# Later column products for two modulation groups, and two slices of the first modulation summed on VectorE

## The chip, the cores and the metric

The kernel runs on one core of a Trainium2 chip. The core has five engines with queues of their own: TensorE (PE, matrix products into PSUM), VectorE (DVE) and ScalarE (ACT) for elementwise work, GpSimd (POOL), and SyncE (SP), whose queue issues the loads and stores here. PE's weight loads are listed apart, as PEld. An engine takes its instructions in the order of its queue, and an instruction that waits holds up all behind it. The metric is the device time of one execution in microseconds (us); smaller is better.

## The reference

One layer of a streaming encoder: a feed-forward block, a token mixer, a second feed-forward block. Each is fed a modulated input, and its result comes back through a gate. All nine modulation vectors are one product of SiLU(c) with `w_ada` (1024 x 9216). x is 512 x 1024, the inner width of a feed-forward is 2816, everything is float32.

```python
sc = jax.nn.silu(c)
mod = sc @ w_ada[l] + b_ada[l]
sh1, s1, g1, sh2, s2, g2, sh3, s3, g3 = jnp.split(mod, N_MOD, axis=-1)
h = _modulate(x, sh1, s1)                       # _rms(x) * (1 + s1) + sh1
x = x + 0.5 * g1[:, None, :] * _swiglu(h, ffn1_w_in[l], ffn1_w_out[l])
h = _modulate(x, sh2, s2)
y = _hybrid_mixer(h, ...)
x = x + g2[:, None, :] * y
h = _modulate(x, sh3, s3)
x = x + 0.5 * g3[:, None, :] * _swiglu(h, ffn2_w_in[l], ffn2_w_out[l])
```

`_swiglu(h, w_in, w_out)` is `(silu(gate) * up) @ w_out` with gate and up the two halves of `h @ w_in`.

## The kernel before, in words

The activations lie transposed in the 128 partitions: eight tiles of 128 channels x 512 tokens. A full-precision product is made of three matmuls on split operands: high x high (L448), low x high (L449) and high x low (L450), 128 x 512 each. Weights come as raw tiles `wr`; ACT casts them to the high part `wh` (L217), DVE subtracts for the low part `wl` (L218). The same split of the modulated input gives `hh` (ACT, L649) and `hl` (DVE, L636), from `hm` (DVE, L647). A unit is one 128-column tile of weights against all eight input tiles: 24 matmuls. A pair of units (gate and up) makes one of 22 tiles f of the inner width.

The first feed-forward begins with phase 0. There the modulation that it needs itself (sh1, s1) is not known yet, and PE makes it as it goes. For each of the eight channel tiles kt there is a slice of `w_ada` of 1 MB (`ar`, 128 x 8 x 2 x 128, two loads) and a weight tile of 384 KB. In group kt, PE first makes the raw columns of kt + 1: small matmuls of 32 columns, packed side by side in the array (`phase0_cols`, L598), which leave partial sums in four partition bands. ACT copies them to `sg` (L601), and two matmuls against a selector, `sel4`, add the bands up into a column each for shift and scale (`columns`, L516). DVE adds the bias (L517, L518) and makes `hm` and `hl` of tile kt + 1, ACT makes `hh`. Between these stand the products of group kt into six accumulators (three tiles f, gate and up). All engines' instructions in phase 0 are tied to the order of the code (`in_order`); elsewhere a scheduler orders them, and the order below is what it gave.

The other modulation groups are summed by DVE beside the products: `ada_rest` loads rows of `w_ada`, scales them by SiLU(c) and adds them up into accumulators `aa` of 128 x 512 (L770 for the first, L772 for each further row tile). What then remains is a sum over partitions. `ada_columns` does it on PE with matmuls against ones, up to four side by side in the array (L791), has ACT copy the result, and transposes it (L798) so that DVE can add the bias (L802) and shift gates (L809). `ada_rest` is a generator, stepped by its caller, `side.step`, after each piece of a product.

- In the first feed-forward, group 0 (g1 and sh2) is stepped through tiles f = 3 to 6, and flushed at the end of f = 6, so its L791 stand there. f = 7 follows, a plain tile with another side job, and then come the products by sevens (L336), which take fewer but combined operands (`tl`, `th`, `sf`, made by DVE and ACT beforehand).
- In the last down projection, group 3 (the last gate; two accumulators) is stepped three times for each part of an output tile. Each of the eight tiles t has three parts (K of 8, 8 and 6 tiles). Tiles 0 and 1 are held in PSUM until the gate is there, then finished (L932), and tile 0 is stored (L1013).

SP issues the loads in order, with at most eight under way; a load also waits until its buffer is free.

Of the kernel before, what the change touches and what calls it, by code (L numbers as in the profile page):

```python
# [11 lines left out]
F32 = mybir.dt.float32  # L12
# [7 lines left out]
P = 128  # L20
# [8 lines left out]
KPARTS = ((0, 8), (8, 8), (16, 6))  # L29
SEVEN = range(8, 19), range(4, 19)  # L30


# [35 lines left out]
class Rates:  # L68


    def __init__(self, sides, rates):
        self.sides, self.rates, self.at = sides, rates, 0

    def step(self, n=1):
# [15 lines left out]
class Block:  # L90
# [51 lines left out]
    @contextmanager  # L142
    def in_order(self, ends=None):

        with self.traced() as block:
            yield
        self.ends = dict(ends or {})
        for i in block:
            if i.engine in self.ends:
                self.follow(i, self.ends[i.engine])  # L150
            self.ends[i.engine] = i.name
# [326 lines left out]
    def phase0(self):  # L478
# [4 lines left out]
        ss = self.const([P, 2 * NB], s="ss")  # L483
        loads = [self.phase0_load(0), self.phase0_load(1)]
        pv = self.aux()
# [26 lines left out]

        def columns(kt, sg, pg):
            k = slice(kt, kt + 1)
            for m in range(2):
                nc.tensor.matmul(pg[:, 256 + m:257 + m], sg[:, m * P:m * P + P], self.sel4, start=True, stop=True)  # L516
            nc.vector.tensor_tensor(out=self.c1[:, k], in0=pg[:, 256:257], in1=self.vT[:, k], op=ALU.add)  # L517
            nc.vector.scalar_tensor_tensor(out=self.c2[:, k], in0=pg[:, 257:258], scalar=1.0, in1=self.vT[:, 8 + kt:9 + kt],  # L518
                                           op0=ALU.add, op1=ALU.add)

        def weights(kt):
            raw, hi, lo = loads[kt][1]
            self.split_w(raw[:, :6, :], hi[:, :6, :], lo[:, :6, :])
            return hi, lo
# [6 lines left out]
        dg = self.diag(r)  # L531
        cols = self.phase0_cols(0, loads[0][0])
        raw0, wh, wl = (x[:, :6, :] for x in loads[0][1])
        w = wh, wl
# [13 lines left out]
        raw(*tiles[7])  # L548
        pu = [self.acc() for _ in range(3)] + [self.aux() for _ in range(3)]
        for kt in range(KT):  # L550
            (hi, lo), (xh, xl) = w, self.h[kt]
            more = kt + 1 < KT
            if kt + 2 < KT:
                loads.append(self.phase0_load(kt + 2))
            if kt == 0:
# [20 lines left out]

    def phase0_load(self, kt):
        a1, win = self.ins["w_ada"][0], self.ins["ffn1_w_in"][0]
        a = self.p0.tile([P, KT, 2, P], F32, tag="ar", name=self.name("ar"))
        w = self.w_tiles()  # L580

        def ada():
            for m in range(2):
                self.load(a[:, :, m, :], a1[:, m * D + kt * P:m * D + (kt + 1) * P].rearrange("(k p) n -> p k n", p=P))

        ada()
        self.loaded = self.load(w[0][:, :6, :].rearrange("p (m j) f -> p m (j f)", m=2),
                  win[kt * P:(kt + 1) * P, :].rearrange("p (m f) -> p m f", m=2)[:, :, :384])
        return a, w

    def phase0_cols(self, kt, a):
# [9 lines left out]
        nc.scalar.copy(sg, pg[:, :256])  # L601
        return sg, pg

# [140 lines left out]
    def ada_rest(self, groups, late=False):  # L744
# [98 lines left out]
    def ffn1(self):  # L843
# [81 lines left out]
    def down(self, act, gate, norm=None):  # L925
# [34 lines left out]
        for t in range(last):  # L960
            if norm and t == 1:
                self.masks()
            for i, _ in enumerate(parts(t, full, late=not norm and t < 2)):
                side.step(2 if norm else 3)
                if t > 2:
                    consts.step()
                if not norm and i == 1 and t > 2:
                    self.store(t - 2, range(NB))
            if not norm and t == 1:
                side.flush()  # L970
                for h in held:
                    finish(*h)
                self.store(0, range(NB))
        side.flush()
# [1158 lines left out]
```

## Time and profile before

| | |
|---|---|
| device time, median of 3 | 1056.32 us (1053.74 to 1056.46) |
| profiled execution | 1056.87 us, span 1055.2 us |
| mean granted TensorE clock | 0.997 |
| PE busy | 1034.8 us, 98% |
| DVE busy | 719.2 us, 68% |
| ACT busy | 487.1 us, 46% |
| PE busy from 60 to 90 us / 90 to 130 / 930 to 955 | 30.00 of 30 / 39.07 of 40 / 23.37 of 25 |
| DVE busy in the same stretches | 25.16 / 34.64 / 14.83 |

Phase 0 lies in the first 60 us, the ones-products of group 0 at 110 to 113 us, those of group 3 at 942 to 946 us. A row of a timeline reads: start in us, duration in us, engine, line, operation, output and inputs, shape and count; in brackets the idle time ahead of it and what ended it. Matmuls overlap in the trace, so the distance between two starts is what one of them costs PE, not its duration. A row of the waits reads: engine and line that waited, what it waited for, us in total, number of waits, longest.

### The profile page before, as it was taken

How to read it: one execution, taken by the hardware profiler on the slowest of the kernel's cores; microseconds unless marked ns; L12 is line 12 of the kernel's file. 1: busy time of each engine (PE TensorE's matmuls, PEld its weight loads, DVE VectorE, ACT ScalarE, POOL GpSimd, SP SyncE). 2: the span in 40 equal slices, each digit the busy share in tenths (PEclk: the TensorE clock that was granted, in tenths of full speed). 3: DMA queues.
4: the chain of work that ended last, by engine and by line, in shares of the span. 5: the costliest groups of instructions: out<-in, count | busy, mean ns of one | idle time of the engine just before them, and what ended most of it. 6: DMA issues, size and time to landing. Idle time of an engine off the chain costs nothing.

```text
span 1055.2 us, 16491 instructions
## 1 busy us (share of the span) xinstructions
PE 1034.8 (98%) x6489; PEld 906.8 (86%) x6489; DVE 719.2 (68%) x1278; ACT 487.1 (46%) x890; POOL 24.9 (2%) x74
## 2 busy tenths in 40 slices
PE   6999999999999999999999989999999999999998
PEld 5788799998887798888788769998999999878888
DVE  4479888767687937558788477788788886663221
ACT  3453455556222225568865554364555556512221
POOL 0000000000000000100000001100000000000000
PEclk8999999999999999999999999999999999999999
DMA  9988333334888635311232021104333344373311
GB/s 275 286 259 274 87 101 104 104 97 127 265 277 276 191 90 161 86 41 41 61 75 71 21 80 41 40 23 119 96 105 101 101 120 118 114 229 92 112 57 40
DMA packets 208028, 130.75 MB, mean 124 GB/s; under 512 B 13889, under 2 KB 192078, under 8 KB 207950
## 3 DMA queue, kind: packets, MB, share of 16 engines
q1 hardware_dynamic: 207950, 129.69, 41.5%
q8 instruction: 51, 0.84, 0.3%
q14 instruction: 27, 0.22, 0.1%
HBM read 127.18 MB, written 2.49 MB: 123 GB/s over the span
## 4 chain that ended last, share of the span: by engine, by line
PE 88%; DVE 6%; issue 2%; DMA 2%; ACT 1%; POOL 0%; SPq 0%; POOLq 0%; ACTq 0%; DVEq 0%
PE pa L448 17%; PE pa L449 16%; PE pa L450 16%; PE pa L336 14%; PE pb L336 11%; DVE aa L772 1%; DMA ar<-in_w_ada 1%; PE pb L1866 1%; PE pb L1846 1%; PE pb L598 1%; PE pb L448 1%; PE pb L449 1%; PE pb L450 1%; PE pb L1466 1%; DVE wl L218 1%
## 5 line engine op out<-in xcount | busy, mean ns | idle before, releaser
L217 ACT CAST wh<-wr 128x1024 fp32r<-128x1024 f32 (+1 forms) x112 | 112.1, 1006 | 221.2 <-PE pa L449 192.9
L218 DVE TENSOR_TENSOR wl<-wr,wh 128x1024 fp32r<-128x1024 f32 (+1 forms) x112 | 130.4, 1168 | 110.8 <-ACT wh L217 106.2
L448 PE MATMUL pa<-hh,wh 128*128 128x512 f32 (+1 forms) x421 | 162.3, 385 | 0.0
L450 PE MATMUL pa<-hh,wl 128*128 128x512 f32 (+1 forms) x421 | 160.4, 381 | 0.0
L449 PE MATMUL pa<-hl,wh 128*128 128x512 f32 (+1 forms) x421 | 160.4, 381 | 0.0
L448 PE MATMUL pa<-ah,wh 128*128 128x512 f32 (+1 forms) x396 | 146.6, 370 | 0.0
L450 PE MATMUL pa<-ah,wl 128*128 128x512 f32 (+1 forms) x396 | 145.4, 367 | 0.0
L449 PE MATMUL pa<-al,wh 128*128 128x512 f32 (+1 forms) x396 | 145.1, 366 | 0.0
L448 PEld LDWEIGHTS pa<-hh,wh 128*128 128x128 f32 x421 | 79.4, 189 | 16.5 <-issue 1.7
L450 PEld LDWEIGHTS pa<-hh,wl 128*128 128x128 f32 x421 | 79.3, 188 | 14.5 <-DVE wl L218 0.4
L449 PEld LDWEIGHTS pa<-hl,wh 128*128 128x128 f32 x421 | 79.4, 189 | 13.1 <-DVE hl L636 0.2
L448 PEld LDWEIGHTS pa<-ah,wh 128*128 128x128 f32 x396 | 74.7, 189 | 14.2 <-ACT wh L217 2.5
L450 PEld LDWEIGHTS pa<-ah,wl 128*128 128x128 f32 x396 | 74.7, 189 | 13.0 <-issue 0.8
L252 DVE TENSOR_TENSOR wl<-sf,wh 128x1024 fp32r<-128x1024 f32 x52 | 63.5, 1221 | 31.7 <-ACT wh L256 31.6
L449 PEld LDWEIGHTS pa<-al,wh 128*128 128x128 f32 x396 | 74.8, 189 | 11.8
L772 DVE SCALAR_TENSOR_TENSOR aa<-ar,sc,aa 128x512 f32<-128x512 f32 x98 | 73.0, 749 | 10.1 <-DMA ar<-in_w_ada 8.6
L336 PE MATMUL pa<-hh,wl 128*128 128x256 f32 x208 | 59.0, 284 | 0.0
L336 PE MATMUL pa<-tl,wh 128*128 128x256 f32 x208 | 59.0, 284 | 0.0
L336 PE MATMUL pa<-th,wl 128*128 128x256 f32 x208 | 59.0, 284 | 0.0
L336 PE MATMUL pa<-th,wh 128*128 128x256 f32 x208 | 59.0, 283 | 0.0
L336 PE MATMUL pa<-hh,wh 128*128 128x256 f32 x208 | 59.0, 283 | 0.0
L336 PE MATMUL pa<-hl,wh 128*128 128x256 f32 x208 | 59.0, 283 | 0.0
(435 smaller groups left out, 2290.3 us busy)
## 6 DMA issues: line engine op xcount, KB each, us to landing
wr<-in_ffn_w_in SPq DMA_DIRECT2D x79, 512.0 KB, 3.9
ar<-in_w_ada SPq DMA_DIRECT2D x80, 256.0 KB, 5.5
ar<-in_w_ada SPq DMA_DIRECT2D x32, 512.0 KB, 6.4
wr<-in_ffn_w_out SPq DMA_DIRECT2D x32, 512.0 KB, 4.1
wr<-in_w_in SPq DMA_DIRECT2D x21, 512.0 KB, 3.7
wr<-in_ffn_w_out SPq DMA_DIRECT2D x16, 384.0 KB, 3.6
wr<-in_w_out SPq DMA_DIRECT2D x8, 512.0 KB, 4.0
wr<-in_ffn_w_in SPq DMA_DIRECT2D x8, 384.0 KB, 8.3
```

What stands on the lines that cost most here:

```text
L217: self.nc.scalar.copy(hi, raw)
L218: self.nc.vector.tensor_tensor(out=lo, in0=raw, in1=hi.bitcast(F32), op=ALU.subtract)
L252: sub = lambda out, x, y: nc.vector.tensor_tensor(out=out, in0=x, in1=y, op=ALU.subtract)
L336: nc.tensor.matmul(z, a[:, j, :], b, start=start and j == 0 and i == 0, stop=j == 3 and i == 2, skip_group_check=not start)
L448: mm(out, wh, xh, start=start, stop=False)
L449: mm(out, wh, xl, start=False, stop=False)
L450: mm(out, wl, xh, start=False, stop=stop)
L598: nc.tensor.matmul(pg[32 * q:32 * q + 32, :256], self.sc[:, kc:kc + 1].to_broadcast([P, 32]), a[:, kc], start=(e == 0), stop=(e == 1), til ...
L772: nc.vector.scalar_tensor_tensor(out=acc, in0=a, scalar=sc, in1=acc, op0=ALU.mult, op1=ALU.add)
L1466: nc.tensor.matmul(pa[:, ps], kh[:, ps], x[:, ps], start=True, stop=True)
L1846: nc.tensor.matmul(ps[:, :n], self.qnT[h][:, ts], self.knT[h][:, :n], start=True, stop=False)
L1866: nc.tensor.matmul(po[:, :P], pT[:, b * P:(b + 1) * P], v[b][:, h * P:(h + 1) * P], start=(b == 0), stop=(b == i))
```

## The change

It has three parts. Line numbers of the changed kernel are higher than those before: L448, L449, L450 become L453, L454, L455; L798 becomes L830, L791 becomes L823; L636 and L647 become L665 and L676; L217 and L218 become L222 and L223.

Part A, phase 0. The slice of a group is loaded one step ahead of its weights. For slices 5 and 7 the matmuls of `phase0_cols` and the copy after them are left out; instead ACT scales the first row tile of the slice (L626) and DVE adds the other seven (L628), 128 x 256 each, and `columns` uses ones for the selector. These are not tied to the order of the code. `columns` of the other slices comes one product earlier in its group, that of the summed ones ahead of the group's first product.

SP's queue from slice 2 on, before (`ar` are slices, `wr` weights):

```order
L128 DMA ar78_262<-in_w_ada 128x8x128 x2
L128 DMA wr79_263<-in_ffn1_w_in 128x2x384
L128 DMA ar87_312<-in_w_ada 128x8x128 x2
L128 DMA wr88_313<-in_ffn1_w_in 128x2x384
L128 DMA ar94_358<-in_w_ada 128x8x128 x2
L128 DMA wr95_359<-in_ffn1_w_in 128x2x384
```

The same queue after, from slice 2 on:

```order
L130 DMA ar24_122<-in_w_ada 128x8x128 x2
L130 DMA ar79_265<-in_w_ada 128x8x128 x2
L130 DMA wr80_268<-in_ffn1_w_in 128x2x384
L130 DMA ar88_315<-in_w_ada 128x8x128 x2
L130 DMA wr89_318<-in_ffn1_w_in 128x2x384
L130 DMA ar95_361<-in_w_ada 128x8x128 x2
```

Slice 3 has moved ahead of the weights of group 2, and so on for each group.

DVE's queue in group 3, before (`hl` of tile 3 at the top, of tile 4 at the bottom):

```order
L636 SCALAR_TENSOR_TENSOR hl55_203<-hm100_388,sh46_194,hh54_202 128x512
L218 TENSOR_TENSOR wl97_361<-wr95_359,wh96_360 128x768
L517 TENSOR_TENSOR sh46_194<-pb105_411,vT26_126 128x1
L518 SCALAR_TENSOR_TENSOR s147_195<-pb105_411,vT26_126 128x1
L647 SCALAR_TENSOR_TENSOR hm107_434<-xT14_106,s147_195,rb82_275 128x512
L636 SCALAR_TENSOR_TENSOR hl57_205<-hm107_434,sh46_194,hh56_204 128x512
```

DVE's queue over the same steps after:

```order
L665 SCALAR_TENSOR_TENSOR hl56_206<-hm101_388,sh47_197,hh55_205 128x512
L628 SCALAR_TENSOR_TENSOR sg106_414<-ar95_361,sc26_127,sg106_414 128x256 x4
L223 TENSOR_TENSOR wl98_366<-wr96_364,wh97_365 128x768
L628 SCALAR_TENSOR_TENSOR sg106_414<-ar95_361,sc26_127,sg106_414 128x256
L526 TENSOR_TENSOR sh47_197<-pb107_423,vT27_129 128x1
L527 SCALAR_TENSOR_TENSOR s148_198<-pb107_423,vT27_129 128x1
L628 SCALAR_TENSOR_TENSOR sg106_414<-ar95_361,sc26_127,sg106_414 128x256
L676 SCALAR_TENSOR_TENSOR hm109_443<-xT14_106,s148_198,rb83_278 128x512
L628 SCALAR_TENSOR_TENSOR sg106_414<-ar95_361,sc26_127,sg106_414 128x256
L665 SCALAR_TENSOR_TENSOR hl58_208<-hm109_443,sh47_197,hh57_207 128x512
```

The seven sums of slice 5 stand between the steps that make tile 4; those of slice 7 stand in group 5, six after `hl` of tile 5 and one after `wl`. On ACT the scaled copy of slice 5 stands right behind `hh` of tile 3.

Part B, first feed-forward. Group 0's ones-products and transposes are stepped from inside f = 7, no longer flushed ahead of it, and its accumulators come from the general slots. PE's queue where they stood before, between f = 6 and f = 7 (f = 6 uses `pa199`; the two units of f = 7 are `pa219` and `pa228` before, `pa215` and `pa226` after):

```order
L449 MATMUL pa199_940<-hl63_211,wh189_891 128x512
L450 MATMUL pa199_940<-hh62_210,wl190_892 128x512
L791 MATMUL pb212_1000<-aa138_652,ones11_97 32x512
L791 MATMUL pb212_1000<-aa159_759,ones11_97 32x512
L791 MATMUL pb212_1000<-aa180_872,ones11_97 32x512
L791 MATMUL pb212_1000<-aa201_971,ones11_97 32x512
L448 MATMUL pa219_1025<-hh48_196,wh197_936 128x512
```

PE's queue after, between the two units of f = 7:

```order
L454 MATMUL pa215_1008<-hl64_214,wh197_934 128x512
L455 MATMUL pa215_1008<-hh63_213,wl198_935 128x512
L823 MATMUL pb222_1049<-aa138_650,ones11_97 32x512
L823 MATMUL pb222_1049<-aa159_757,ones11_97 32x512
L823 MATMUL pb222_1049<-aa180_870,ones11_97 32x512
L823 MATMUL pb222_1049<-aa201_969,ones11_97 32x512
L453 MATMUL pa226_1060<-hh49_199,wh213_1004 128x512
```

They have moved by one unit, from the end of f = 6 to the middle of f = 7; the four transposes move from four matmuls behind them to the end of f = 7. On DVE the first sum of the group now stands behind three further `wl` and the three products `af` of f = 0 to 2, and on SP the fourth load of the group stands behind three more weight tiles.

Part C, last down projection. The sums are stepped twice per part instead of three times; the held tiles are finished after the first part of t = 2, tile 0 is stored after its second. PE's queue before (the sums' second accumulator is `aa1930` before, `aa1933` after):

```order
L450 MATMUL pa1942_9993<-ah1862_9662,wl1937_9960 128x512
L791 MATMUL pb1946_10024<-aa1918_9889,ones11_97 32x512
L448 MATMUL pa1942_9993<-ah1872_9693,wh1944_9996 128x512
L449 MATMUL pa1942_9993<-al1873_9694,wh1944_9996 128x512
L791 MATMUL pb1946_10024<-aa1930_9944,ones11_97 32x512
L450 MATMUL pa1942_9993<-ah1872_9693,wl1945_9997 128x512
```

PE's queue after, at the end of tile 1:

```order
L454 MATMUL pa1938_9979<-al1913_9853,wh1947_10024 128x512
L455 MATMUL pa1938_9979<-ah1912_9852,wl1948_10025 128x512
L823 MATMUL pb1952_10076<-aa1918_9887,ones11_97 32x512
L823 MATMUL pb1952_10076<-aa1933_9966,ones11_97 32x512
L453 MATMUL pa1954_10081<-ah1844_9589,wh1950_10054 128x512
L454 MATMUL pa1954_10081<-al1845_9590,wh1950_10054 128x512
```

The two stand next to each other, at the end of tile 1 (`pa1938`), 39 product matmuls later. Between phase 0's end and the last down projection, apart from part B, all engines keep their order.

```diff
+SUMMED = (5, 7)
...
     def in_order(self, ends=None):
+        self.loose = set()
         with self.traced() as block:
             yield
         self.ends = dict(ends or {})
         for i in block:
+            if i.name in self.loose:
+                continue
             if i.engine in self.ends:
...
-        loads = [self.phase0_load(0), self.phase0_load(1)]
+        slices, parts = [], []
+        for kt in range(3):
+            slices.append(self.phase0_slice(kt))
+            if kt < 2:
+                parts.append(self.phase0_weights(kt))
...
+            if kt + 3 < KT:
+                slices.append(self.phase0_slice(kt + 3))
             if kt + 2 < KT:
-                loads.append(self.phase0_load(kt + 2))
+                parts.append(self.phase0_weights(kt + 2))
...
             for j in range(6):
+                if j == 0 and kt + 2 in SUMMED:
+                    sums[kt + 2] = self.phase0_sums(slices[kt + 2])
                 if j == 0 and more:
-                    cols = self.phase0_cols(kt + 1, loads[kt + 1][0])
+                    if kt + 1 in SUMMED:
+                        cols = sums[kt + 1], self.aux(), self.ones[:, 0:1]
+                    else:
+                        cols = self.phase0_cols(kt + 1, slices[kt + 1])
                     if kt > 0:
                         w = weights(kt + 1)
-                if j == 2 and more:
+                if j == (kt + 1 not in SUMMED) and more:
                     columns(kt + 1, *cols)
...
+    def phase0_sums(self, a):
+        nc = self.nc
+        sg = self.slot(s="sg")[:, :256]
+        with self.traced() as block:
+            nc.scalar.activation(sg, a[:, 0], AF.Copy, scale=self.sc[:, 0:1])
+            for kc in range(1, KT):
+                nc.vector.scalar_tensor_tensor(out=sg, in0=a[:, kc], scalar=self.sc[:, kc:kc + 1], in1=sg, op0=ALU.mult,
+                                               op1=ALU.add)
+        self.loose.update(i.name for i in block)
+        return sg
...
-                acc = self.slot(s="aa") if late else self.early.tile([P, NT], F32, tag="aa", name=self.name("aa"), bufs=6)
+                acc = self.slot(s="aa")
...
             waiting = self.ada_columns(g, accs)
+        if not late:
+            self.columns = waiting
+            return
         yield
         yield
...
         self.seven_enter()
-        self.plain(act, 7, 8, sums, True)
+        side.add(self.columns)
+        self.plain(act, 7, 8, Rates((sums, side), (1, 0.1)), True)
         sums.flush()
+        side.flush()
         self.by_sevens(act, SEVEN[0])
...
-                side.step(2 if norm else 3)
+                side.step(2)
...
-                if not norm and i == 1 and t > 2:
-                    self.store(t - 2, range(NB))
-            if not norm and t == 1:
-                side.flush()
-                for h in held:
-                    finish(*h)
-                self.store(0, range(NB))
+                if not norm and t > 2:
+                    if i == 1:
+                        self.store(t - 2, range(NB))
+                elif not norm and t == 2:
+                    if i == 0:
+                        side.flush()
+                        for h in held:
+                            finish(*h)
+                    elif i == 1:
+                        self.store(0, range(NB))
```

More of the change, by code (lines that the diff above doesn't have):

```diff
@@ L72, in __init__ @@
         self.sides, self.rates, self.at = sides, rates, 0
+        self.add = sides[0].add
     def step(self, n=1):
@@ L511, in phase0, with columns @@
         self.new_h()
-        def columns(kt, sg, pg):
+        def columns(kt, sg, pg, ones):
             k = slice(kt, kt + 1)
             for m in range(2):
-                nc.tensor.matmul(pg[:, 256 + m:257 + m], sg[:, m * P:m * P + P], self.sel4, start=True, stop=True)
+                nc.tensor.matmul(pg[:, 256 + m:257 + m], sg[:, m * P:m * P + P], ones, start=True, stop=True)
             nc.vector.tensor_tensor(out=self.c1[:, k], in0=pg[:, 256:257], in1=self.vT[:, k], op=ALU.add)
@@ L521, in weights @@
         def weights(kt):
-            raw, hi, lo = loads[kt][1]
+            raw, hi, lo = parts[kt]
             self.split_w(raw[:, :6, :], hi[:, :6, :], lo[:, :6, :])
@@ L531, in phase0 @@
         dg = self.diag(r)
-        cols = self.phase0_cols(0, loads[0][0])
-        raw0, wh, wl = (x[:, :6, :] for x in loads[0][1])
+        cols = self.phase0_cols(0, slices[0])
+        raw0, wh, wl = (x[:, :6, :] for x in parts[0])
         w = wh, wl
@@ L549, in phase0 @@
         pu = [self.acc() for _ in range(3)] + [self.aux() for _ in range(3)]
+        sums = {}
         for kt in range(KT):
@@ L575, in phase0, with phase0_slice, phase0_weights @@
         return pu
-    def phase0_load(self, kt):
-        a1, win = self.ins["w_ada"][0], self.ins["ffn1_w_in"][0]
+    def phase0_slice(self, kt):
+        a1 = self.ins["w_ada"][0]
         a = self.p0.tile([P, KT, 2, P], F32, tag="ar", name=self.name("ar"))
+        for m in range(2):
+            self.load(a[:, :, m, :], a1[:, m * D + kt * P:m * D + (kt + 1) * P].rearrange("(k p) n -> p k n", p=P))
+        return a
+    def phase0_weights(self, kt):
         w = self.w_tiles()
[L582 to L586, printed above, removed]
+        win = self.ins["ffn1_w_in"][0]
         self.loaded = self.load(w[0][:, :6, :].rearrange("p (m j) f -> p m (j f)", m=2),
                   win[kt * P:(kt + 1) * P, :].rearrange("p (m f) -> p m f", m=2)[:, :, :384])
-        return a, w
+        return w
     def phase0_cols(self, kt, a):
@@ L601, in phase0_cols @@
         nc.scalar.copy(sg, pg[:, :256])
-        return sg, pg
+        return sg, pg, self.sel4
+    def phase0_sums(self, a):
[8 more added lines that the diff above has]
+        return sg
     def new_h(self):
```

## The prediction, made before the changed kernel ran

> **What bounds the kernel now.** I read the busy shares first, then the slices, the chain that ended last, the waits of PE, and the timelines of PE, VectorE (DVE), ScalarE (ACT) and SP at the three places of the change.
>
> ```profile
> PE 1034.8 (98%) x6489; PEld 906.8 (86%) x6489; DVE 719.2 (68%) x1278; ACT 487.1 (46%) x890; POOL 24.9 (2%) x74
> PE   6999999999999999999999989999999999999998
> PE 88%; DVE 6%; issue 2%; DMA 2%; ACT 1%; POOL 0%; SPq 0%; POOLq 0%; ACTq 0%; DVEq 0%
> PE pb L791 <- DVE aa L772: 2.6, 2, 1.6
> ```
>
> PE fills nearly every slice and carries 88% of the chain, so time moves in two ways only: work taken off PE, one for one, or a gap of PE that opens or closes. The last row (us in total, times, longest) names two such gaps of 2.6 us together: PE stands at the ones-products until DVE has ended the sums of a modulation group. The change touches both, and phase 0.
>
> **Part A, phase 0: slices 5 and 7 summed by DVE.** A k-group of phase 0 on PE before (start, duration, both us):
>
> ```profile
> 35.52 0.39 PE L450 MATMUL pa<-hh,wl 128*128 128x512 f32 x1
> 35.76 0.50 PE L516 MATMUL pb<-sel,sg 128*128 128x1 f32 x4
> 36.44 0.39 PE L449 MATMUL pa<-hl,wh 128*128 128x512 f32 x1
> 38.48 0.39 PE L449 MATMUL pb<-hl,wh 128*128 128x512 f32 x1
> 38.70 0.39 PE L450 MATMUL pb<-hh,wl 128*128 128x512 f32 x1
> 39.02 1.09 PE L598 MATMUL pb<-ar,sc 128*32 128x256 f32 x16
> 40.38 0.40 PE L449 MATMUL pa<-hl,wh 128*128 128x512 f32 x1
> ```
>
> Ordinary matmuls start 0.227 us apart (nine steps from 36.44 to 38.48, the rows between left out). From L450 at 38.70 to L449 at 40.38 are 1.68 us, with two ordinary steps in it (0.455): an L598 block costs PE 1.22 us. Two go: -2.44. The pair of L516 stays, with ones for the selector, at its cost of 0.92 - 0.455 = 0.465 (35.52 to 36.44).
>
> For each of the two slices come one scaled copy on ACT, which replaces the copy of L601, and seven multiply-adds on DVE:
>
> ```profile
> L647 DVE SCALAR_TENSOR_TENSOR hm<-xT,mod,pb 128x256 f32<-128x256 f32 x32 | 14.9, 475 | 2.8 <-PE pb L622 2.8
> 37.48 0.72 ACT L649 ACTIVATE hh<-hm,sh 128x512 fp32r<-128x512 f32 x1 [1.95 <-DVE hm L647]
> 40.21 0.37 ACT L601 COPY sg<-pb 128x256 f32<-128x256 f32 x1 [0.46 <-PE pb L598]
> 40.48 0.84 ACT L217 CAST wh<-wr 128x768 fp32r<-128x768 f32 x1
> 38.24 0.75 DVE L636 SCALAR_TENSOR_TENSOR hl<-hm,sh,hh 128x512 fp32r<-128x512 f32 x1 [0.79 <-ACT hh L649]
> 41.35 0.96 DVE L218 TENSOR_TENSOR wl<-wr,wh 128x768 fp32r<-128x768 f32 x1 [2.36 <-ACT wh L217]
> 44.02 0.75 DVE L636 SCALAR_TENSOR_TENSOR hl<-hm,sh,hh 128x512 fp32r<-128x512 f32 x1 [0.79 <-ACT hh L649]
> ```
>
> By the first row (mean 475 ns) the 14 take 6.7 us. A group lasts 5.78 us (hl to hl), of which DVE has work for under 2.9, so the room is there; what counts is the queue. Group 3 in the new order: hl ends at 39.0, four sums to 40.9, wl still behind its cast to 42.2, a sum to 42.7, the two small adds to 42.9, a sum to 43.4, hm (0.75, as hl) to 44.1, a sum to 44.6, hl from 44.9 (behind its hh) to 45.6; it ended at 44.8. PE begins the next group at 39.02 + 5.78 - 0.2 (below) = 44.6 with the ones-pair and reads hl as its second matmul at about 45.3: a wait of some 0.35 us. The same working at group 5 (six sums, wl, one sum) gives 0.15. Bounds: 0, if every step is a little shorter; 1.2, if each handover costs 0.1 us more.
>
> [...]
>
> Columns that stay on PE move up by one product. That closes a wait of a weight load at group 1:
>
> ```profile
> PEld pa L450 <- DVE wl L218: 0.4, 1, 0.4
> 28.50 0.40 PE L449 MATMUL pa<-hl,wh 128*128 128x512 f32 x1
> 28.91 0.50 PE L450 MATMUL pa<-hh,wl 128*128 128x512 f32 x1
> ```
>
> The step is 0.41 instead of 0.227: -0.2. In exchange the copy of sg (to 40.58 above) has one product less ahead of L516, which would start at 40.38 + 2 x 0.227 = 40.84 with its weight load ahead of it. It just fits; I charge 0.04 in each of five groups, 0.2 (0 to 0.75).
>
> The loads: slice k+3 now goes ahead of the weights of k+2 on SP's one queue.
>
> ```profile
> 17.55 2.37 SPq L128 DMA_DIRECT2D wr<-in_ffn_w_in  x1
> 22.35 2.33 SPq L128 DMA_DIRECT2D wr<-in_ffn_w_in  x1
> wr<-in_ffn_w_in SPq DMA_DIRECT2D x1, 384.0 KB, 8.3
> 28.60 0.84 ACT L217 CAST wh<-wr 128x768 fp32r<-128x768 f32 x1
> ```
>
> The third row is for the second: weights 3, taken up at 22.35, landed at 30.65. Weights 2 (before: 17.55) will have one 384 KB load less ahead of them than these had, worth 1.3 us at 300 GB/s (282 over the first 33 us, in a row below, the first two of them empty), and land at 29.35: 0.75 us behind the cast at 28.60. Cast, wl, adds, hm, hh, hl then end at 33.75, and PE reads that hl at about 34.4 (40.38 - 5.78 - 0.2): covered, by 0.65. If that cover goes, PE waits one for one. In the new order slices 4 and 5 (2.1 MB) come behind all that weights 3 had ahead of them before: 30.65 + 7.0 = 37.7. ACT comes to the scaled copy of slice 5 at 38.2, behind its hh (37.48 + 0.72). Covered by 0.5.
>
> Part A: -2.44 - 0.2 + 0.35 + 0.15 + 0.2 = **-1.9** (-2.6 to -0.7).
>
> **Part B, first feed-forward: the four ones-products one unit later.** Before, and then the same block where nothing waits:
>
> ```profile
> 109.44 0.39 PE L450 MATMUL pa<-hh,wl 128*128 128x512 f32 x1
> 109.76 1.06 PE L791 MATMUL pb<-aa,ones 128*32 128x512 f32 x6
> 111.75 1.05 PE L791 MATMUL pb<-aa,ones 128*32 128x512 f32 x2 [0.93 <-DVE aa L772]
> 113.06 0.39 PE L449 MATMUL pa<-hl,wh 128*128 128x512 f32 x1
> 317.83 0.39 PE L450 MATMUL pa<-ah,wl 128*128 128x512 f32 x1
> 318.15 1.07 PE L791 MATMUL pb<-aa,ones 128*32 128x512 f32 x8
> 319.49 0.39 PE L449 MATMUL pa<-al,wh 128*128 128x512 f32 x1
> ```
>
> 3.62 us against 1.66 for the same work: the wait costs 1.96. It is 0.93 of idling and the second start of a block. After, L791 stands 24 matmuls (5.45 us) later, on a PE that is 1.9 ahead: at 109.76 - 1.9 + 5.45 = 113.3. DVE's last sums ended at 109.37 + 2.32 = 111.7:
>
> ```profile
> 109.37 2.32 DVE L772 SCALAR_TENSOR_TENSOR aa<-ar,sc,aa 128x512 f32<-128x512 f32 x3
> 0.00:33.00 33.00, 24.45 (x135) 18.38 (x135) 15.69 (x36) 13.55 (x29) 2.34 (x12) 0.90 1.00 282
> 90.00:130.00 40.00, 39.07 (x197) 31.70 (x196) 34.64 (x56) 13.88 (x20) 0.00 (x0) 1.00 0.52 165
> ```
>
> The windows' columns are length, then busy time of PE, PEld, DVE, ACT, POOL, clock, DMA share, GB/s. DVE is busy 34.64 of 40 us from 90 to 130: the stretch where the sums could be late. Their order also changes (three wl ahead of the first sum, the fourth load of sums behind three more weights), but their work does not. So the slack is about 1.6 us, and a lateness beyond that is paid one for one: -1.96 is taken, 0 is the other end. Four transposes (L798) only move along.
>
> **Part C, last down projection: both ones-products together, 39 matmuls later.**
>
> ```profile
> 942.05 0.39 PE L450 MATMUL pa<-ah,wl 128*128 128x512 f32 x1
> 942.37 1.04 PE L791 MATMUL pb<-aa,ones 128*32 128x512 f32 x2
> 945.71 1.04 PE L791 MATMUL pb<-aa,ones 128*32 128x512 f32 x2 [1.63 <-DVE aa L772]
> 947.02 0.39 PE L448 MATMUL pa<-ah,wh 128*128 128x512 f32 x1
> 941.76 3.90 DVE L772 SCALAR_TENSOR_TENSOR aa<-ar,sc,aa 128x512 f32<-128x512 f32 x5 [1.45 <-DMA ar<-in_w_ada]
> ```
>
> Four ordinary steps take 4.97 us here instead of 0.91: 4.06 go. One block at the new place costs 1.66 - 0.455 = 1.2. Net **-2.9**. The sums end at 945.7; the pair now stands at 942.37 + 39 x 0.227 = 951.2, so 5.5 us cover a lateness. If the 1.63 of idling came back, -1.3 would be left. Finishing tiles 0 and 1 and their store come later by one part, with three down tiles to follow: nothing.
>
> Sum: -1.9 - 2.0 - 2.9 = -6.8. The rows are of an execution of 1056.87 us, 0.55 above the median of 1056.32; I apply the sum to the median: **1049.5**.
>
> **The rivals.** (1) One wait stays: DVE, pressed from 60 to 130, is late at L791 again or holds up what follows (sevens' operands), or several waits of phase 0 grow to their bounds: 2 to 3 us of the gain go, 1051.5 to 1053. Against it: the slack of 1.6 us. (2) The change does not do what it says: in phase 0 the sums only trade PE's block for DVE's lateness (+1.2 and +0.75 on the groups, weights 2 late), and part B only moves its wait: -6.8 + 1.2 + 2 + 1 = -2.6, about 1053.7, no change. (3) Slower: ACT is a strict queue, and the scaled copy of slice 5 or 7 stands on it ahead of hm, sg, the weight cast and hh of the next group. If the slice has not landed when ACT comes to it, all of these are late and PE waits one for one. The copy is reached at 38.2; the price is the lateness less the room of about 0.5 up to there, for each slice. To turn -6.8 into +3.5 takes 5.7 us of lateness on both: 1060. The loads moved at one rate through all of phase 0 before, and I see no source for that much.
>
> **How the numbers follow.** Forecast 0.72, rival 1 0.14, rival 2 0.06, rival 3 0.08. The range: down to 1047.5 (all costs at their good ends, -7.5, and 1.3 for half the spread of the runs shown, 1053.74 to 1056.46), up to 1053.2, the upper end of rival 1. Within 0.3% (3.2 us) a measurement of this kernel can hardly tell a change. Faster by more than that: 0.72 + 0.14 = 0.86; same 0.06; slower 0.08.
>
> **What would show it.** Part A: 96 passes of L598 for 128, phase 0 shorter by 1.9 us, waits of under 0.5 us on hl or sg. Part B: no wait at the ones-products, the block near 113 us. Part C: one block near 947 us on the new clock (951.2 - 3.9), no wait. Wrong would make it a row of ACT at the scaled copy with a DMA as its releaser, or a wait on sums that stays.

## The result, and the profile after

The changed kernel takes 1050.28 us in the median of ten executions (1049.60 to 1052.49), against 1056.20 of the kernel before beside it: a ratio of 0.9955, with a 95% interval of 0.9942 to 0.9968, that is 3.4 to 6.1 us less. That is under 1%, but the interval leaves out 1: it is faster, by a little less than forecast. Run a second time, beside other executions of the kernel before, it took 1049.81 against 1056.70, a ratio of 0.9941 (0.9925 to 0.9957).

The profiled execution took 1051.66 us, with a span of 1049.9 where it was 1055.2. Busy shares and chain of its page:

```profile
PE 1030.7 (98%) x6457; PEld 906.0 (86%) x6457; DVE 725.9 (69%) x1292; ACT 487.3 (46%) x890; POOL 24.9 (2%) x74
PE 93%; DVE 3%; issue 1%; DMA 1%; SPq 0%; POOL 0%; ACT 0%; POOLq 0%
```

PE has 32 passes less (two blocks of 16) and 4.1 us less busy time, DVE 14 instructions and 6.7 us more. To see where the span went, I compare the start of the same instruction in both traces. PE's timeline of the kernel before, at group 0 of phase 0, behind phase 0, at the first product by sevens, behind the mixer's recurrence, and in the last down projection after part C:

```profile
22.69 1.09 PE L598 MATMUL pb<-ar,sc 128*32 128x256 f32 x16
59.24 0.48 PE L448 MATMUL pa<-hh,wh 128*128 128x512 f32 x1
124.20 0.28 PE L336 MATMUL pa<-hh,wh 128*128 128x256 f32 x1
640.75 0.39 PE L448 MATMUL pa<-mh,wh 128*128 128x512 f32 x1
969.44 0.39 PE L449 MATMUL pa<-al,wh 128*128 128x512 f32 x1
```

The same five in the changed kernel, and its two blocks of ones-products:

```profile
23.34 1.09 PE L615 MATMUL pb<-ar,sc 128*32 128x256 f32 x16
57.64 0.40 PE L453 MATMUL pa<-hh,wh 128*128 128x512 f32 x1
113.51 1.07 PE L823 MATMUL pb<-aa,ones 128*32 128x512 f32 x8
120.45 0.36 PE L341 MATMUL pa<-hh,wh 128*128 128x256 f32 x1
638.35 0.39 PE L453 MATMUL pa<-mh,wh 128*128 128x512 f32 x1
949.49 1.05 PE L823 MATMUL pb<-aa,ones 128*32 128x512 f32 x4
964.17 0.39 PE L454 MATMUL pa<-al,wh 128*128 128x512 f32 x1
```

| stretch | difference at its start, us | at its end | change | forecast |
|---|---|---|---|---|
| set-up | 0 | +0.65 | +0.65 | 0 |
| phase 0 (part A) | +0.65 | -1.60 | -2.25 | -1.9 |
| to the sevens (part B) | -1.60 | -3.75 | -2.15 | -2.0 |
| to behind the mixer | -3.75 | -2.40 | +1.35 | 0 |
| last down projection (part C) | -2.40 | -5.27 | -2.87 | -2.9 |

The three parts bring 7.3 us in this pair of traces; 2.0 us are given back in two places that the change does not touch. At the second, in the mixer, the order of all engines is that of before. Of its 1.35 us, 0.38 are gone by 620 us, in small steps (PE is then 3.37 us ahead); the other 0.97 come from 626 us on. What differs there is the clock (windows of the changed kernel: busy time of PE, its weight load, DVE, ACT and POOL with their instructions, then the granted clock, the DMA share and GB/s):

```profile
14.00:24.00 10.00, 8.64 (x48) 5.85 (x52) 5.47 (x16) 2.47 (x4) 0.00 (x0) 0.66 1.14 306
624.00:626.00 2.00, 0.34 (x2) 0.15 (x2) 2.00 (x4) 2.00 (x4) 0.00 (x0) 1.00 0.00 0
626.00:628.00 2.00, 1.93 (x12) 1.77 (x13) 2.00 (x4) 0.80 (x2) 0.00 (x0) 0.78 0.00 0
628.00:630.00 2.00, 2.00 (x12) 2.00 (x11) 1.28 (x3) 0.59 (x1) 0.00 (x0) 0.50 0.00 0
630.00:632.00 2.00, 2.00 (x17) 2.00 (x17) 1.89 (x3) 0.58 (x1) 0.00 (x0) 0.87 0.76 221
```

For 3.4 us in all the clock was granted in half ((0.22 + 0.50 + 0.13) x 2 / 0.5). Just ahead of this PE waits 1.66 us for DVE (PE's timeline, changed kernel):

```profile
625.88 3.22 PE L1655 MATMUL pb<-vb,U 128*128 128x128 f32 x16 [1.66 <-DVE vb L1235]
```

In the profiled execution before, the same products stand behind the same wait, and the clock stayed at 1.00 (PE's timeline; then the windows of the kernel before, with the row of its start):

```profile
629.25 2.33 PE L1618 MATMUL pb<-vb,U 128*128 128x128 f32 x16 [1.65 <-DVE vb L1198]
14.00:24.00 10.00, 9.25 (x53) 6.12 (x54) 4.88 (x14) 2.63 (x5) 0.00 (x0) 0.66 1.13 311
628.00:630.00 2.00, 0.75 (x7) 0.78 (x7) 2.00 (x4) 1.59 (x3) 0.00 (x0) 1.00 0.00 0
630.00:632.00 2.00, 1.93 (x18) 1.77 (x17) 2.00 (x4) 0.97 (x2) 0.00 (x0) 1.00 0.00 0
```

So the length of the gap, 1.66 us against 1.65, is not what makes the difference between these two.

The 0.65 us in the set-up, ahead of every step of the change, is for the most part the clock as well. The mean from 14 to 24 us is the same, 0.66, but the halved stretch ends later in the changed kernel. PE is 0.09 us behind when it begins the last two products of the set-up; they take 1.03 us before and 1.59 in the changed kernel (PE's timeline and a window, before, then changed):

```profile
21.73 1.03 PE L622 MATMUL pb<-dg,ones 128*128 128x512 f32 x2
22.00:23.00 1.00, 1.00 (x10) 0.25 (x12) 0.00 (x0) 0.20 (x1) 0.00 (x0) 1.00 1.14 306
21.82 1.59 PE L651 MATMUL pb<-dg,ones 128*128 128x512 f32 x2
22.00:23.00 1.00, 1.00 (x3) 0.16 (x1) 0.00 (x0) 0.00 (x0) 0.00 (x0) 0.52 1.16 288
```

### The profile page after: what moved, and what is told of

Its sections match the earlier page's. It is cut to its first block, busy times and chain, and to the rows that moved or that the text cites. A ratio compares the mean times of both kernels' runs of the same rounds, so it can differ in the third digit from the quotient of the medians.

```text
span 1049.9 us, 16450 instructions
## 1 busy us (share of the span) xinstructions
PE 1030.7 (98%) x6457; PEld 906.0 (86%) x6457; DVE 725.9 (69%) x1292; ACT 487.3 (46%) x890; POOL 24.9 (2%) x74
## 4 chain that ended last, share of the span: by engine, by line
PE 93%; DVE 3%; issue 1%; DMA 1%; SPq 0%; POOL 0%; ACT 0%; POOLq 0%
PE pa L453 18%; PE pa L454 18%; PE pa L455 18%; PE pa L341 14%; PE pb L341 11%; PE pb L1903 1%; PE pb L453 1%; PE pb L454 1%; PE pb L455 1%; PE pb L1883 1%; PE pb L1503 1%; DMA ar<-in_w_ada 1%; PE pb L615 1%; PE pb L1455 1%; PE pb L1655 0%
## 5 line engine op out<-in xcount | busy, mean ns | idle before, releaser
L222 ACT CAST wh<-wr 128x1024 fp32r<-128x1024 f32 (+1 forms) x112 | 112.0, 1006 | 229.2 <-PE pa L454 201.2
L223 DVE TENSOR_TENSOR wl<-wr,wh 128x1024 fp32r<-128x1024 f32 (+1 forms) x112 | 130.4, 1169 | 104.1 <-ACT wh L222 101.8
L453 PE MATMUL pa<-hh,wh 128*128 128x512 f32 (+1 forms) x421 | 161.9, 384 | 0.0
L454 PE MATMUL pa<-hl,wh 128*128 128x512 f32 (+1 forms) x421 | 160.2, 381 | 0.0
L455 PE MATMUL pa<-hh,wl 128*128 128x512 f32 (+1 forms) x421 | 160.1, 380 | 0.0
L453 PE MATMUL pa<-ah,wh 128*128 128x512 f32 (+1 forms) x396 | 146.5, 370 | 0.0
L455 PE MATMUL pa<-ah,wl 128*128 128x512 f32 (+1 forms) x396 | 145.1, 366 | 0.0
L454 PE MATMUL pa<-al,wh 128*128 128x512 f32 (+1 forms) x396 | 144.9, 366 | 0.0
L453 PEld LDWEIGHTS pa<-hh,wh 128*128 128x128 f32 x421 | 79.3, 188 | 15.7 <-issue 1.7
L455 PEld LDWEIGHTS pa<-hh,wl 128*128 128x128 f32 x421 | 79.3, 188 | 14.1
L454 PEld LDWEIGHTS pa<-hl,wh 128*128 128x128 f32 x421 | 79.4, 188 | 13.4 <-DVE hl L665 0.2
L453 PEld LDWEIGHTS pa<-ah,wh 128*128 128x128 f32 x396 | 74.7, 189 | 14.3 <-ACT wh L222 2.5
L455 PEld LDWEIGHTS pa<-ah,wl 128*128 128x128 f32 x396 | 74.7, 189 | 12.1
L454 PEld LDWEIGHTS pa<-al,wh 128*128 128x128 f32 x396 | 74.7, 189 | 11.9
```

The lines of the kernel that those rows point to most:

```text
L222: self.nc.scalar.copy(hi, raw)
L223: self.nc.vector.tensor_tensor(out=lo, in0=raw, in1=hi.bitcast(F32), op=ALU.subtract)
L453: mm(out, wh, xh, start=start, stop=False)
L454: mm(out, wh, xl, start=False, stop=False)
L455: mm(out, wl, xh, start=False, stop=stop)
```

## The experiments

Each kernel was run in five rounds beside the kernel before. Time is the median of its executions; the ratio is to the kernel before, run beside it.

### The three parts, each alone

Each of these three is the kernel before with one part of the diff shown above, told here by its functions, and no other line:

```
 a_only: SUMMED, in_order, phase0, phase0_slice, phase0_weights, phase0_cols, phase0_sums
 b_only: ada_rest, ffn1, Rates.add
 c_only: down
```

> Part A alone on the kernel before. If the parts act only through PE and add up: phase 0 ends 1.6 to 2.2 us earlier (two blocks of 1.22 us, less about 0.2 us of waiting at group 4 and 0.2 us at group 0), and the time falls by 1.5 to 2.2 us; the wait at the ones-products of the first feed-forward grows, because PE comes there earlier while VectorE's last sums do not, so that at the start of the sevens only 0 to 1 us of it may be left. If instead part A only trades PE's block for VectorE's lateness, phase 0 ends within 0.5 us of before and the time is unchanged.

> Part B alone. If the parts add up: no wait at the four ones-products, and the sevens start 1.9 to 2.2 us earlier than before; the time falls by about 2 us. If the gain is given back behind it (operands of the sevens late, or accumulators held longer), the sevens start less than 1 us earlier and the time stays within 1 us.

> Part C alone. If the parts add up: one block of ones-products, no wait, and the last down projection is 2.8 to 2.9 us shorter; the time falls by about 2.9 us. If finishing tiles 0 and 1 later costs something at the end, the last down projection is shorter by under 2 us.

| kernel | median, us | before | ratio (95%) | the part's own stretch in its trace |
|---|---|---|---|---|
| a_only | 1054.49 | 1056.43 | 0.9983 (0.9973 to 0.9994) | phase 0: +1.55 to -0.70, -2.25 us |
| b_only | 1054.83 | 1056.43 | 0.9983 (0.9972 to 0.9993) | phase 0's end to the sevens: -1.28 to -3.35, -2.07 us |
| c_only | 1053.24 | 1056.43 | 0.9974 (0.9963 to 0.9985) | last down projection: -2.72 to -5.60, -2.88 us |

Each part alone gains, and its own stretch shrinks by what it shrinks by in the whole. The three ratios make 6.3 us together, each with some 1.1 us of uncertainty; the whole makes 4.8 (3.4 to 6.1) and 6.2 (4.5 to 7.9). So they add up, and nothing points to one part eating another's gain. One expectation of these three was a miss: in the kernel with part A alone I expected the wait at the ones-products to take most of its gain back. The wait is there (waits of PE in that kernel):

```profile
PE pb L820 <- DVE aa L801: 1.0, 1, 1.0
```

but it is no longer than the 0.93 before. DVE's sums came earlier together with PE, so the lead of phase 0 was kept, as -0.70, up to the down projection.

### Which half of part A counts: the blocks

```diff
-SUMMED = (5, 7)
+SUMMED = ()
```

> The changed kernel with no slice summed by VectorE (all eight by PE as before), the order of the loads, the earlier columns and parts B and C kept. If the two blocks of PE are what part A gains: phase 0 ends 2.0 to 2.3 us later than in the changed kernel, and the time is 1.8 to 2.4 us above it. If the order of the loads or the earlier columns bring part of the gain, the difference is under 1.5 us.

Measured: 1052.70 us, 2.4 above the first runs of the changed kernel and 2.9 above the second. Its ratio to the kernel before is 0.9970 (0.9960 to 0.9981), which makes the difference 1.6 and 3.1 us by the two ratios of the changed kernel. So the two blocks are the gain of part A, as far as these intervals tell. The trace showed something else. This execution began with a full clock, PE was at group 0 2.5 us earlier than in the trace before, and of this 1.5 us were gone at the end of phase 0. One reason stands in ScalarE's timeline:

```profile
28.25 0.84 ACT L222 CAST wh<-wr 128x768 fp32r<-128x768 f32 x1 [1.89 <-DMA wr<-in_ffn_w_in]
```

That is the cast of the weights of group 2, which the prediction had down as covered by 0.65 us. It does not wait in the profiled execution of the changed kernel, where the clock at the start is halved and PE is late; it does here, where PE is 2 us ahead.

### The clock at the start, and the order of the loads

```diff
         for i in (4, 5, 6):
             raw(*tiles[i])
+        pw = self.aux()
+        for i in range(14):
+            nc.tensor.matmul(pw[:, :P], self.ident, self.ones, start=True, stop=True)
```

This fills PE's wait of 2.4 to 3.7 us ahead of phase 0 with products that nothing reads: in the kernel before (warm_before), in the changed one (warm), and in the changed one with slices 2 to 4 loaded behind the weights of the group before, as they were (warm5). loads5 has that order of loads without the added products:

```diff
-        for kt in range(3):
+        for kt in range(2):
             slices.append(self.phase0_slice(kt))
-            if kt < 2:
-                parts.append(self.phase0_weights(kt))
+            parts.append(self.phase0_weights(kt))
...
-            if kt + 3 < KT:
+            if kt < 3:
+                slices.append(self.phase0_slice(kt + 2))
+            if 2 <= kt < KT - 3:
                 slices.append(self.phase0_slice(kt + 3))
```

> The kernel before with 14 added products of two constants on PE (nothing reads them) in the 3 us in which PE waits for VectorE ahead of phase 0. Theory: the spread of the runs (1053 to 1058) comes from whether the clock is granted in full or in half between about 14 and 24 us, and that hangs on the idling before it. Then the profile shows a granted clock of 1.00 from about 10 us on, phase 0 starts 1.5 to 2.5 us earlier than in the profiled execution before, most runs lie at 1053 to 1054.5 and the median is 1.5 to 2.5 us lower. If the spread comes from elsewhere (loads, the mixer), the median stays within 1 us, or rises by up to 1 us through the added work.

> The changed kernel with the same 14 added products. If the two effects simply add, the median falls by 2 us to about 1048.3. Theory: with a full clock PE comes to group 2 some 2 us earlier, and the weights of group 2, which now land behind slice 3, are then late (28.3 us): ScalarE's cast waits 1 to 2 us on that load, PE stands about 1.2 us in groups 1 to 3, and the median falls by only about 1 us, to 1049 to 1049.5.

> The same, with the slices ahead of the weights only from slice 5 on (slices 2 to 4 stay behind the weights of the group before, as in the kernel before). If the late weights of group 2 take the gain, they are on time here, the cast does not wait on a load, and the time is about 1 us under that of the kernel with the added products alone: near 1048.2. If the order of the loads does not matter, the two are equal.

> The changed kernel with the slices ahead only from slice 5 on, without added products. In executions whose clock is halved at the start nothing is late in either order, so the time is that of the changed kernel; in those with a full clock it is about 1 us lower. Median 0 to 0.8 us under the changed kernel (1049.5 to 1050.3).

| kernel | median, us | ratio (95%) |
|---|---|---|
| warm_before | 1056.73 (before: 1055.66) | 1.0001 (0.9986 to 1.0015) |
| warm | 1050.26 | 0.9939 (0.9919 to 0.9959) |
| warm5 | 1049.81 | 0.9940 (0.9919 to 0.9961) |
| loads5 | 1050.51 | 0.9941 (0.9921 to 0.9961) |

With the added products the profiled executions of all three have the clock at 1.00 from 12 us on (means of the executions 0.999, 1.000 and 1.000), but five of the eleven profiled executions without them had it too from 14 us on. That the clock hangs on the idling ahead of it was my guess, and is not shown by this. Nor does the time follow the clock here. The theory behind warm_before, a median 1.5 to 2.5 us lower, did not hold, and warm (1049 to 1049.5 expected), warm5 (near 1048.2) and loads5 (1049.5 to 1050.3) all came out above what was expected. In warm_before PE came to group 0 1.9 us earlier, was 0.9 us earlier at the end of phase 0 and 0.25 us a unit later. VectorE's timeline shows where it went:

```profile
47.89 0.75 DVE L639 SCALAR_TENSOR_TENSOR hl<-hm,sh,hh 128x512 fp32r<-128x512 f32 x1 [0.79 <-ACT hh L652]
53.14 0.17 DVE L1344 COPY ex<-vb 128x4 f32<-128x4 f32 x1 [4.50 <-DMA vb<-in_gdn_a_log]
53.23 0.96 DVE L218 TENSOR_TENSOR wl<-wr,wh 128x768 fp32r<-128x768 f32 x1
```

A copy of four columns, with nothing to do with phase 0, waits 4.5 us for a load of 2 KB that stands behind all the weights on SP's queue, and the split of a weight tile waits behind it. c_only, which has the phase 0 of before, also began with a full clock. There the same copy waits 1.02 us, and of a lead of 2.2 us at group 0 1.8 are left a unit behind phase 0. So a full clock at the start does not by itself make a shorter execution: how much of the lead survives hangs on a load. In warm ScalarE's cast waits 2.2 us on the weights of group 2, a little more than expected; in warm5 that wait is gone, and instead the scaled copy of slice 5 waits 0.8 and another cast 0.7. The four times lie within what their intervals allow.

The clock does go with the time of single executions, though. Each has a mean granted clock on record; the 64 executions of the kernel before that were run beside these experiments fall apart like this:

| mean granted clock | executions | median, us | lowest to highest |
|---|---|---|---|
| 0.998 to 1.000 | 34 | 1055.53 | 1053.89 to 1057.92 |
| 0.996 and 0.997 | 15 | 1056.87 | 1055.64 to 1059.16 |
| 0.995 and less | 15 | 1058.73 | 1056.41 to 1064.67 |

So much of the spread of the kernel before goes with the clock. Where in an execution it was halved is known only for the profiled ones, and what spreads those of the first row over some 4 us stays open.

### The loads of the summed slices

old_loads undoes the order of the loads and keeps the sums; late_slices puts the load of a summed slice behind two weight tiles more; after_again is the changed kernel itself. The order of loads in phase 0, slices (s) and weights (w):

```
 old_loads:   s0 w0 s1 w1 s2 w2 s3 w3 s4 w4 s5 w5 s6 w6 s7 w7
 late_slices: s0 w0 s1 w1 s2 s3 w2 s4 w3 w4 w5 s5 s6 w6 w7 s7
 changed:     s0 w0 s1 w1 s2 s3 w2 s4 w3 s5 w4 s6 w5 s7 w6 w7
```

> The changed kernel with each slice loaded right ahead of its own group's weights, as before; the two sums stay. Slice 5 then lands 1.3 us later than in the changed kernel, about 39.0 against 38.2 at which ScalarE comes to it, and the weights of group 2 are 3.5 us earlier. If the loads ahead are needed for the sums, the scaled copy waits 0.5 to 2 us and the median is 0.5 to 1.5 us higher than that of the changed kernel; if not, it is equal or up to 0.5 us lower.

> The changed kernel with the loads of slices 5 and 7 issued behind the weights of groups 4 and 5, and of 6 and 7: slice 5 lands about 2.6 us later than in the changed kernel. If ScalarE's queue behind the scaled copy sets the price one for one: the scaled copy waits 1 to 3 us on its load, hm, hh and hl of tile 4 come that much later, PE stands 1.5 to 2.5 us at the start of group 4, and the median rises by 1.5 to 2.5 us to about 1052.3. If VectorE and ScalarE have room for it, it rises by less than 0.5 us.

> The changed kernel once more, as it is, beside the three below and with new runs of the kernel before. If the gain of 6 us between the medians is real: 1049.5 to 1051 and a ratio of 0.994 to 0.995. In an execution with a full clock at the start, ScalarE's cast of the weights of group 2 waits 1.5 to 2.2 us on their load.

| kernel | median, us | ratio (95%) | phase 0 in its trace, start to end |
|---|---|---|---|
| after_again | 1049.81 | 0.9941 (0.9925 to 0.9957) | -2.45 to -2.34, +0.1 us |
| old_loads | 1050.68 | 0.9948 (0.9934 to 0.9963) | -2.21 to -1.83, +0.4 us |
| late_slices | 1051.07 | 0.9957 (0.9941 to 0.9973) | -2.57 to -1.52, +1.0 us |

All three profiled executions began with a full clock. The changed kernel's cast of the weights of group 2, in ScalarE's timeline of after_again (in brackets: us idle ahead of it, and what ended that):

```profile
26.00 0.37 ACT L618 COPY sg<-pb 128x256 f32<-128x256 f32 x1 [0.94 <-PE pb L615]
29.32 0.84 ACT L222 CAST wh<-wr 128x768 fp32r<-128x768 f32 x1 [2.95 <-DMA wr<-in_ffn_w_in]
```

The weights landed at 29.3, to the tenth where the prediction had put them (29.35). The tenth is luck: in no_sums, with the same order of loads, they landed at 28.25, in warm at 28.9. But ScalarE stood there from 26.4 on, a wait longer than the 1.5 to 2.2 us expected, and PE's lead on the trace before falls from 2.5 us to 0.2 in groups 1 to 3. In the order of before, the same cast in c_only, with a full clock too, waits for no load (ScalarE's timeline):

```profile
26.36 0.84 ACT L217 CAST wh<-wr 128x768 fp32r<-128x768 f32 x1
```

The trace before had a halved clock at its start, so it is no fair measure of part A here. The profiled executions that began with a full clock are, all as differences to the trace before:

| trace | phase 0 | start | end | a unit later |
|---|---|---|---|---|
| c_only | as before | -2.22 | -2.26 | -1.76 |
| warm_before | as before | -1.91 | -0.91 | -0.25 |
| no_sums | new order of loads, no sums | -2.48 | -0.99 | -1.03 |
| after_again | changed | -2.45 | -2.34 | -2.44 |
| warm | changed | -2.11 | -2.79 | -2.88 |

"A unit later" is the product that starts at 65.24 us in the trace before. Behind a halved clock part A shortens phase 0 by 2.25 us. Behind a full one, from start to a unit later, after_again is 0.5 us shorter than c_only, and warm 2.4 us shorter than warm_before. With one trace of each kernel, more than these two ends can't be said.

In old_loads the place of the wait has changed (ScalarE's timeline):

```profile
35.09 0.73 ACT L676 ACTIVATE hh<-hm,sh 128x512 fp32r<-128x512 f32 x1 [1.94 <-DVE hm L674]
38.91 0.51 ACT L624 ACTIVATE sg<-ar,sc 128x256 f32<-128x256 f32 x1 [3.09 <-DMA ar<-in_w_ada]
39.33 0.71 ACT L308 ACTIVATE hm<-hm,sh 128x512 f32<-128x512 f32 x1
39.94 0.35 ACT L616 COPY sg<-pb 128x256 f32<-128x256 f32 x1
40.19 0.83 ACT L222 CAST wh<-wr 128x768 fp32r<-128x768 f32 x1
```

Slice 5 lands at 38.9 (expected: 39.0), the scaled copy waits 3.09 us for it, and `hm`, `sg` and the cast stand behind it. Of these 3.09 us PE sees 1.7, in its wait for `sg` (waits of PE in old_loads: total us, how many, the longest):

```profile
PE pb L524 <- ACT sg L616: 1.7, 1, 1.7
```

In late_slices the copy waits 0.73 us until 39.9 (and 0.50 for slice 7), and the sums are ready too late for their ones-products (waits of PE in late_slices):

```profile
PE pb L525 <- ACT sg L623: 1.4, 2, 1.1
PE pb L525 <- DVE sg L633: 0.6, 1, 0.6
```

So the mechanism of the third rival exists, in both forms. Its price is not one for one on ScalarE's wait, as I had it: 1.7 of 3.09. It costs 0.9 us of phase 0 in late_slices beside after_again, and 1.3 us in the medians, where 1.5 to 2.5 were expected. Between the orders the medians differ by 0.9 and 1.3 us, inside their intervals.

### A third slice

```diff
-SUMMED = (5, 7)
+SUMMED = (3, 5, 7)
```

> The changed kernel with slices 3, 5 and 7 summed by VectorE. One block more off PE is worth 1.22 us. Slice 3 is due at ScalarE at about 26 us, lands at 27 to 28 and stands ahead of the cast of the weights of group 2. Theory: the block is gained and half of it is lost to waits on that load; the median is 0.3 to 0.9 us under the changed kernel. Rival: the wait on the load costs all of it, and the median is 0 to 2 us higher.

Measured: 1053.25 us, ratio 0.9970 (0.9954 to 0.9986), 3.4 us above the changed kernel run beside it. The rival is right, and by more than its price. In its trace, whose start had 3.4 us of halved clock, phase 0 gains nothing against the trace before (-0.29 to -0.32) although three blocks are off PE. ScalarE's timeline:

```profile
28.05 0.51 ACT L626 ACTIVATE sg<-ar,sc 128x256 f32<-128x256 f32 x1 [0.82 <-DMA ar<-in_w_ada]
29.03 0.83 ACT L222 CAST wh<-wr 128x768 fp32r<-128x768 f32 x1 [0.21 <-DMA wr<-in_ffn_w_in]
32.61 0.72 ACT L678 ACTIVATE hh<-hm,sh 128x512 fp32r<-128x512 f32 x1 [2.75 <-DVE hm L676]
35.22 0.83 ACT L222 CAST wh<-wr 128x768 fp32r<-128x768 f32 x1 [1.89 <-DMA wr<-in_ffn_w_in]
```

The copy waits for slice 3, `hh` for DVE's sums, and the cast of weights 3 for their load. A further 3 us in this trace went at two places of the mixer where the order is unchanged: DVE's maximum of a softmax came 1.7 us late, and a load from DRAM (`t<-t_d`) took 3.3 us of waiting against 1.95. Whether that belongs to this kernel or to this execution was not settled.

No kernel tried is faster than the changed one by more than the intervals.

## Why the prediction was right

The predicted 1049.5 us lies 0.8 below the measured 1050.28 and within the range, and each part did by its own mechanism what it was expected to.

- **Part A's blocks.** The step of 1.22 us for a block holds within the noise: without the sums the median is 2.4 to 2.9 us higher (1.6 to 3.1 by the ratios), for 2.44 forecast.
- **Part A's waits.** Too high. The queue of VectorE in group 3 ran as worked out: four sums from 39.38, `hl` of tile 4 at 45.20 on a clock that was 0.5 us late. PE lost under 0.2 us there, where 0.35 were put down. PE's timeline of the changed kernel there, `pb` by `sg` being the ones-products of `sg`:

```profile
45.04 0.39 PE L455 MATMUL pb<-hh,wl 128*128 128x512 f32 x1
45.27 0.50 PE L525 MATMUL pb<-ones,sg 128*128 128x1 f32 x4
45.63 0.48 PE L453 MATMUL pa<-hh,wh 128*128 128x512 f32 x1
46.01 0.50 PE L454 MATMUL pa<-hl,wh 128*128 128x512 f32 x1
```

  And DVE's:

```profile
39.38 2.04 DVE L628 SCALAR_TENSOR_TENSOR sg<-ar,sc,sg 128x256 f32<-128x256 f32 x4
45.20 0.75 DVE L665 SCALAR_TENSOR_TENSOR hl<-hm,sh,hh 128x512 fp32r<-128x512 f32 x1 [0.40 <-ACT hh L678]
```

  The sums took 0.51 us each in a row of four (2.04), near the 0.475 of the row that the prediction took them from. The wait of 0.15 at group 6 and the 0.04 for the copy of `sg` in each group did not come; the earlier columns cost 0.2 once, at group 0, and brought 0.25 at group 1.
- **Weights of group 2: "covered, by 0.65".** The landing was about right, the cover was not a property of the kernel. It came from an execution whose clock was halved from about 15 to 22 us; the 0.90 for the first 33 us stands in the prediction's own row, and nothing was made of it. With a full clock ScalarE is there 2 to 3 us before the load (no_sums, warm, after_again). This is the term that was mis-sized: no wait in the profiled execution with a halved clock at the start; 2.95 us of ScalarE and 2.3 of PE in after_again, 2.2 and 1.5 in warm, both with a full one.
- **Part B.** Forecast -1.96, measured -2.15, alone -2.07: the wait was the cost, as forecast. The block stands at 113.51, where 113.3 was forecast, and no wait is left. The pressed VectorE (first rival) did not show.
- **Part C.** Forecast -2.9, measured -2.87 and -2.88 alone. The block came at 949.5, not near 947, since PE was only 2.4 us ahead at that stage, not 3.9.
- **The sum.** It was held against the median as if the rest of the kernel stood still. In the profiled pair it did not: +0.65 us in the set-up and +1.35 in the mixer, most of both with the clock. The total is 4.8 and 6.2 us by the two ratios, not 6.8; that the median came within 0.8 us of the forecast is in part luck.
- **Rivals.** The second (the sums only trade PE's block for lateness) is most of what happens within phase 0 in after_again, with a full clock, and what happens to three slices in the one trace of three_sums; it does not hold for the whole change, because parts B and C do not depend on it. The third was given 0.08 with "no source for that much": its source is a start at full clock, and in the orders of loads tried its size stays near 1 us.

## What to carry to other kernels

A wait that PE meets once, for sums that another engine will have ready a unit later, was worth its whole idling plus the second start of the block at both places here (2 to 2.9 us), and moving the consumer back, with other products on the queue between, was as cheap as it looked (-2.15 and -2.87 us measured, -1.96 and -2.9 forecast). A cover worked out from one profile is a cover on that execution's clock: before trusting a slack near the start of a kernel, work it out a second time for the fastest start; here PE was at phase 0 1.9 to 2.6 us earlier with a full clock, and the weights of group 2 landed at 28.25 to 29.3 us all the same, where 29.35 had been worked out from the execution with the halved one. Moving work off the bounding engine paid here until its inputs came too late, and that point was one slice away: behind a halved clock two slices gained 2.25 us in phase 0, three gained nothing (0.03).

## What the runs showed of the hardware

The granted clock of PE is not a constant of the kernel. In the traces of before and after it was 1.00 or, for stretches, 0.50: from 14 to 24 us the mean is 0.66 in both, which is 6.8 us of halved clock. In a_only it was 0.50 through the whole of these 10 us (mean of the execution 0.995); in after_again and c_only it was 1.00 there. The lengths of halved clock that were met are 3.4 us, 6.8 us and some 10 us.

In four traces a short gap was followed by half clock. A wait of PE of 1.63 to 1.66 us in the mixer was followed by 3.4 us of it in both traces of the changed kernel and in those of loads5 and old_loads; a wait of the same length was not in the other ten. All four are of kernels with parts B and C; of these, five kept the full clock, as did all five without. What decides between the two outcomes, and whether the change makes one likelier, no run here shows.

Filling PE's wait with 14 useless products went with a clock of 1.00 at the start in every one of the three profiled executions, as in five of the eleven without them, and gained no time that could be measured; in warm_before a load of 2 KB held VectorE for 4.5 us instead.
